# A batched fp32 matmul: the first block of x comes in two halves, one over each DMA queue

## The chip, the cores and the metric

The kernel runs on one core of a Trainium2 chip. The time is device microseconds of that core for one execution, and a kernel's time is the median of its runs. A profile is one execution recorded by the hardware profiler; its times are counted from the span's start.

## The reference

```python
def setup_inputs():
    batch, m, k, n = 32, 512, 1024, 768
    return {
        "x": np.random.randn(batch, m, k).astype(np.float32),
        "weight": np.random.randn(batch, k, n).astype(np.float32),
    }

def reference(x, weight):
    return np.matmul(x, weight).astype(np.float32)
```

There are 32 independent products of a 512 x 1024 matrix with a 1024 x 768 matrix, all in fp32 in HBM. The kernel multiplies in bf16 and sums in fp32.

## The kernel before, in words

**Tiling.** Batches are taken in 16 pairs. The x of one pair (4 MB in fp32) lies over the 128 partitions so that partitions 0 to 63 hold the pair's first batch and partitions 64 to 127 its second (`x_view`, L39). Each partition holds 8 rows of 1024 numbers, which are contiguous in HBM; the 8 rows are the index `mo`. A weight matrix (3 MB in fp32) lies over the 128 partitions with 8 x 768 numbers on each (L37, L38). There are two slots for the x of a pair (`xs`), four for weights (`ws`), and four for results (`outs`, one per pair).

**Loads.** x and weights are wanted in bf16. GpSimd's queue, the software queue, converts while it moves: `load_w` (L93) and `load_x` (L108) read fp32 from HBM and write bf16 to SBUF. The one exception is the x of the first pair. SyncE loads it over the hardware queue, unconverted, into a piece of the result buffer that is not yet in use (`x_first`, L53; issued at L393), and VectorE and ScalarE convert it into `xs[0]`: `cast_first` (L275) lets each engine wait for `s_first` and copy four of the eight `mo`; ScalarE's last copy also waits for `s_cast`, which VectorE raises after its four, and then raises `s_xr`, on which TensorE waits before it touches a pair's x.

**TensorE** (`on_pe`, L192). For each pair: 8 groups of 4 transposes (L174, x seen as 32-bit words, with the identity `ident` as the other operand), which VectorE copies out of PSUM into `both` (`spread`, L217); then for each of the two batches a wait for its weights (`s_wr`) and 4 x 8 pairs of matmuls (L139 and L166). ScalarE (L262, L266) and VectorE (L271, L273) copy the sums out of PSUM into `outs`.

**Order on GpSimd** (`on_pool`, L342). First `load_w(0)`; then the identity (a memset, L344, and an affine_select, L346); then `load_w(1)`, `load_x(1)`, `load_w(2)`, `load_w(3)`. After that, in one fixed order, each later load waits until TensorE has freed its slot, and the stores of finished pairs (L119) are put between the loads, some pairs after their results are ready. ScalarE waits for the store of a slot before it writes it again (`slot_free`, L231). SyncE stores the last two pairs, the last one in four pieces (L376 to L379), and waits for the weights to land on TensorE's behalf (L340).

The two helpers around the first load, as they stand before the change:

```python
def cast_first(eng, copy, rows):
    eng.wait_ge(s_first, 16)
    for mo in rows:
        if mo == 2 * MT - 1:
            eng.wait_ge(s_cast, 1)
        last = copy(xs[0][:, mo], x_first[:, mo])
    return last
...
sp.dma_start(x_first, x_view[0]).then_inc(s_first, 16)
```

Of the kernel before, what the change touches and what calls it, by code (L numbers as in the profile page):

```python
# [12 lines left out]
def kernel(  # L13
# [10 lines left out]
    H = P // 2  # L24
# [10 lines left out]
    pe, dve, act, pool, sp = nc.tensor, nc.vector, nc.scalar, nc.gpsimd, nc.sync  # L35
# [3 lines left out]
    x_view = x.rearrange("(p r) (mi mo) k -> p (r mi) mo k", r=2, mo=2 * MT)  # L39
# [3 lines left out]
    def sbuf(name, shape, dtype):  # L43
        return nc.alloc_sbuf_tensor(name, shape, dtype).ap()

    ident = sbuf("ident", [P, P], F32)
    all_ws = sbuf("w", [P, W_SLOTS // 2, 2, KT, N], BF16)
    ws = [all_ws[:, i // 2, i % 2] for i in range(W_SLOTS)]
    xs = [sbuf(f"x{i}", [P, 2 * MT, K], BF16) for i in range(X_SLOTS)]
# [3 lines left out]
    x_first = all_outs[:, 4 * ROW:4 * ROW + 2 * MT * K].rearrange("p (mo k) -> p mo k", mo=2 * MT)  # L53
# [7 lines left out]
    def sem(name):  # L61
        sems.append(nc.alloc_semaphore(name))
        return sems[-1]

    s_first, s_cast, s_zero, s_ident = (sem(f"s_{n}") for n in ("first", "cast", "zero", "ident"))
    s_w = [sem(f"s_w{i}") for i in range(W_SLOTS)]
    s_x = [sem(f"s_x{i}") for i in range(X_SLOTS)]
    s_wr, s_xr = sem("s_wr"), sem("s_xr")
# [7 lines left out]
    def mm_done(b):  # L76
        return 4 * (b + 1)
# [12 lines left out]
    def together(b):  # L90
        return W_SLOTS <= b < B - 2

    def load_w(b):  # L93
        if together(b):
            if b % 2 == 0:
                pool.wait_ge(s_mm, mm_done(b + 1 - W_SLOTS))
                slots = all_ws[:, b // 2 % 2].rearrange("p r ko n -> p r (ko n)")
                pool.dma_start(out=slots, in_=w_two_view[b // 2]).then_inc(s_w[b % W_SLOTS], 16)  # L98
            return
        if b >= W_SLOTS:  # L100
            pool.wait_ge(s_mm, mm_done(b - W_SLOTS))
        pool.dma_start(out=ws[b % W_SLOTS], in_=w_view[b]).then_inc(s_w[b % W_SLOTS], 16)  # L102
# [5 lines left out]
    def load_x(k):  # L108
        if k >= X_SLOTS:
            pool.wait_ge(s_mm, mm_begun(k - X_SLOTS))  # L110
        pool.dma_start(out=xs[k % X_SLOTS], in_=x_view[k]).then_inc(s_x[k % X_SLOTS], 16)  # L111
# [5 lines left out]
    def store(eng, a, sem):  # L117
        copied(eng, 4 * a + 3)
        eng.dma_start(out=two_view[a], in_=outs[a % OUT_SLOTS]).then_inc(sem, 16)  # L119
# [72 lines left out]
    def on_pe():  # L192


        odd = pe.alloc_register("odd")
        pe.reg_mov(odd, 0)
        pe.wait_ge(s_ident, 1)
        with nc.Fori(0, PAIRS, engines=[mybir.EngineType.PE], hint_back_edge=True):
            take(s_xr)
            for k in range(X_SLOTS):  # L200
                with pe.If_eq(odd, k):
                    transposes(k)
            w_pair = all_ws[:, bass.ds(nc.snap(odd, min_val=0, max_val=1), 1)]
            for b in range(2):
                take(s_wr)
                for mt in range(MT):
                    if b == 0:
                        await_copies(s_c, 2 * mt + 2, GROUPS, GROUPS)
                    at = 2 * b + mt // 2 + 1 + mt % 2
                    await_copies(s_a, at, 5, 4)  # L210
                    await_copies(s_d, at, 5, 4)
                    multiply(b, mt, w_pair[:, 0, b])
            pe.reg_alu(odd, odd, 1, mybir.AluOpType.bitwise_xor)
# [61 lines left out]
    def cast_first(eng, copy, rows):  # L275

        eng.wait_ge(s_first, 16)
        for mo in rows:
            if mo == 2 * MT - 1:
                eng.wait_ge(s_cast, 1)  # L280
            last = copy(xs[0][:, mo], x_first[:, mo])  # L281
        return last

    def on_dve():


        turn = dve.alloc_register("turn")
        dve.reg_mov(turn, 0)
        dve.sem_inc(s_d, 2)
        dve.sem_inc(s_free, OUT_SLOTS)  # L290
        cast_first(dve, dve.tensor_copy, range(MT)).then_inc(s_cast, 1)
        turns = PAIRS // OUT_SLOTS

        def spreads(k, copy):
            for g in range(GROUPS):
                dve.wait_ge(s_pt, GROUPS * k + g + 1)
                copy(g).then_inc(s_c, 1)

        def sets(b):
            dve.wait_ge(s_free, 1).then_inc(s_free, -1)  # L300
            set_on_dve(b, 0)
            set_on_dve(b, 1)
            set_on_dve(b + 1, 0)

        with nc.Fori(0, turns, engines=[mybir.EngineType.DVE], hint_back_edge=True):
            for k in range(OUT_SLOTS - 1):
                spreads(k, spread)
                if k:
                    set_on_dve(2 * k - 1, 1)
                else:  # L310
                    with dve.If_ne(turn, 0):
                        set_on_dve(2 * OUT_SLOTS - 1, 1)
                sets(2 * k)
            k = OUT_SLOTS - 1
            with dve.If_ne(turn, turns - 1):
                spreads(k, spread)
            with dve.If_eq(turn, turns - 1):
                spreads(k, spread_last)
            set_on_dve(2 * k - 1, 1)
            with dve.If_ne(turn, turns - 1):  # L320
                sets(2 * k)
            with dve.If_eq(turn, turns - 1):
                sets(B - 2)
            step = GROUPS * OUT_SLOTS
            dve.wait_ge(s_pt, step).then_inc(s_pt, -step)
            dve.reg_add(turn, turn, 1)
        set_on_dve(B - 1, 1)

    def on_act():
        act.sem_inc(s_a, 2)  # L330
        cast_first(act, act.copy, range(MT, 2 * MT)).then_inc(s_xr, 1)
        for b in range(B):
            out_on_act(b, 0)
            if b % 2 and b < B - 1:
                landed(act, s_x[(b // 2 + 1) % X_SLOTS], (b // 2 + 2) // 2, s_xr)
            out_on_act(b, 1)
# [3 lines left out]
        eng.wait_ge(slot, 16 * n).then_inc(ready, uses)  # L340

    def on_pool():  # L342
        load_w(0)
        pool.memset(ident, 0.0).then_inc(s_zero, 1)  # L344
        pool.wait_ge(s_zero, 1)
        pool.affine_select(  # L346
            out=ident,
            in_=ident,
            compare_op=mybir.AluOpType.not_equal,
            fill=1.0,  # L350
            base=0,
            pattern=[[-1, P]],
            channel_multiplier=1,
        ).then_inc(s_ident, 1)
        load_w(1)
        load_x(1)
        load_w(2)
        load_w(3)
        def stores(first, last):
            for a in range(max(first, 0), last):  # L360
                store(pool, a, s_st[a % OUT_SLOTS])


        for k in range(PAIRS - 2):
            load_x(k + 2)
            if k % 2 == 0:
                stores(k - 3, k - 1)
            load_w(2 * k + 4)
            load_w(2 * k + 5)
        stores(PAIRS - 3 - HELD, PAIRS - 2)  # L370

    def on_sp():
        for b in range(B):
            if not (together(b) and b % 2):
                landed(sp, s_w[b % W_SLOTS], loads_of_w(b), s_wr, 1 + together(b))
        store(sp, PAIRS - 2, s_fin)  # L376
        for b in (B - 2, B - 1):
            for p in range(2):
                store_half(b, p)  # L379
        sp.sem_inc(s_zero, 1)  # L380

    def clear_on_pool():

        for i, s in enumerate(s_st):
            pool.wait_ge(s, 16 * len(range(i, PAIRS - 2, OUT_SLOTS)))
        pool.wait_ge(s_zero, 2)
        used = range(sems[0].num, s_fin.num)
        pool.dma_reset(used)
        pool.sem_clear(used)
        pool.wait_ge(s_fin, 80).then_inc(s_fin, -80)  # L390

    with tc.tile_critical(sync_engine=mybir.EngineType.Activation, no_gpsimd_drain=True):  # L392
        sp.dma_start(x_first, x_view[0]).then_inc(s_first, 16)  # L393
        on_pool()
        on_pe()
        on_dve()
        on_act()
        on_sp()
        clear_on_pool()
# [30 lines left out]
```

## Time and profile before

| what | before |
|---|---|
| median of 3 runs | 512.89 us (512.43 to 513.11) |
| span of the profiled execution | 510.1 us |
| instructions in the span | 5783 |
| TensorE busy | 422.5 us |
| VectorE busy | 212.8 us |
| ScalarE busy | 115.8 us |
| GpSimd busy | 29.0 us |
| mean granted TensorE clock | 0.951 |

The span runs from the first to the last instruction that the profiler recorded. The device time of the profiled execution is not listed by itself; the median of the runs is 2.8 us longer than the span, and that much is taken to lie around it. "DMA share" in a view by windows is the mean busy share of the core's 16 DMA engines (it can pass 1 in a short window, where packets overlap or are put down to the window they began in). GB/s are counted in the bytes as they are written, so a load that converts fp32 to bf16 counts half of what it reads. "PEq", "SPq" and so on are an engine's sequencer. In the DMA rows the tile names tell the transfer: `outs<-in_x_dram` is the first load of x, since `x_first` lies in the result buffer.

### The profile page before, as it was taken

To read this page: it belongs to the slowest core of one execution; us is meant where nothing else is said; L and a number is where in the kernel's file an instruction comes from. 1 tells how busy PE (TensorE), PEld (TensorE's weight loads), DVE (VectorE), ACT (ScalarE), POOL (GpSimd) and SP (SyncE) were. 2 spreads that over 40 slices of the span, in tenths; PEclk is the share of its full clock that TensorE was granted. 3 is DMA by queue.
4 is the path that set the end of the run, shared out by engine and by line. 5 is a ranking of instruction groups with operands and counts; after the bars stand their busy time and mean duration, and the time that the engine had idled before them with its cause. 6 is when DMAs were issued, how large, how long until landed. Compare 5 with 4: busy or idle time off the path is not lost. (4 is left out here: it accounts for less than half of the span.)

```text
span 510.1 us, 5783 instructions
## 1 busy us (share of the span) xinstructions
PE 422.5 (83%) x2512; PEld 172.3 (34%) x1536; DVE 212.8 (42%) x332; ACT 115.8 (23%) x197; POOL 29.0 (6%) x54
## 2 busy tenths in 40 slices
PE   0199999999999599993999939999499984999990
PEld 0143425353525134251343403434144331343420
DVE  0253636454536136351463513635145441454631
ACT  1313131313231221302313023130222302223130
POOL 2000001000100001000010000100001000100000
PEclk9999999999999899997999969999799995999996
DMA  8999999999999999999999999999999999999997
GB/s 296 261 213 216 217 215 220 212 299 251 214 217 224 432 241 218 215 229 432 233 219 216 244 432 216 220 216 259 419 216 218 219 272 405 215 215 236 434 427 336
DMA packets 9443, 136.34 MB, mean 267 GB/s; under 512 B 864, under 2 KB 864, under 8 KB 1376
## 3 DMA queue, kind: packets, MB, share of 16 engines
q0 software_dynamic: 8576, 125.83, 95.7%
q1 hardware_dynamic: 864, 10.49, 5.0%
q14 instruction: 3, 0.02, 0.0%
HBM read 167.77 MB, written 50.33 MB: 428 GB/s over the span
## 5 line engine op out<-in xcount | busy, mean ns | idle before, releaser
L166 PE MATMUL pm<-w,xT 128*128 x976 | 328.2, 386 | 36.3 <-DVE outs L271 36.3
L139 PE MATMUL pm<-w,xT 128*128 x1024 | 283.9, 277 | 4.7 <-DVE xT L220 1.7
L166 PEld LDWEIGHTS pm<-w,xT 128*128 128x128 bf16 x1024 | 101.8, 99 | 275.4 <-issue 235.8
L271 DVE COPY outs<-pm 64x512 f32<-64x512 f32 x128 | 88.1, 688 | 199.8 <-DVEq L269 198.4
L262 ACT COPY outs<-pm 64x512 f32<-64x512 f32 x128 | 74.1, 579 | 264.1 <-PE pm L139 163.2
L174 PE MATMUL pt<-ident,x 128*128 128x128 f32 x512 | 84.5, 307 | 33.4 <-PEq L178 23.1
L220 DVE COPY xT<-pt 128x1024 bf16<-128x1024 bf16 x120 | 77.8, 687 | 63.4 <-PE pt L174 63.0
L174 PEld LDWEIGHTS pt<-ident,x 128*128 128x128 f32 x512 | 71.2, 210 | 48.7 <-issue 26.5
L266 ACT COPY outs<-pm 64x512 f32<-64x512 f32 x64 | 37.0, 578 | 99.9 <-PE pm L139 99.8
L273 DVE COPY outs<-pm 64x512 f32<-64x512 f32 x64 | 43.9, 685 | 0.0
L98 POOL DMA_DIRECT2D w<-in_weight_dram x13 | 9.2, 706 | 260.0 <-PE pm L139 260.0
L111 POOL DMA_DIRECT2D x<-in_x_dram x15 | 8.3, 555 | 127.3 <-PE pm L139 88.7
L281 DVE CAST x<-outs 128x1024 bf16<-128x1024 f32 x4 | 2.5, 690 | 18.9 <-DMA outs<-in_x_dram 18.9
L119 POOL DMA_DIRECT2D out_dram<-outs x14 | 7.5, 537 | 7.1 <-DVE outs L273 7.1
L281 ACT CAST x<-outs 128x1024 bf16<-128x1024 f32 x4 | 3.9, 1042 | 16.6 <-DMA outs<-in_x_dram 16.6
L228 DVE COPY xT<-pt 128x512 bf16<-128x512 bf16 x16 | 5.7, 418 | 4.1 <-PE pt L174 4.1
L102 POOL DMA_DIRECT2D w<-in_weight_dram x6 | 3.4, 564 | 29.1 <-PE pm L139 27.9
L281 ACT ACT_TABLE_LOAD x1 | 1.3, 1283 | 1.0 <-ACTq L392 1.0
L346 POOL TENSOR_SCALAR_AFFINE_SELECT ident<-ident 128x128 f32<-128x128 f32 x1 | 0.3, 282 | 0.2 <-POOL ident L344 0.2
L344 POOL MEMSET ident<- 128x128 f32 x1 | 0.2, 223 | 0.0
L414 POOL MEMSET const-float32-0.0<- 128x1 f32 x1 | 0.1, 98 | 0.2 <-issue 0.2
L414 POOL MEMSET const-bfloat16-1.0<- 128x1 bf16 x1 | 0.1, 102 | 0.0
(2 smaller groups left out, 0.2 us busy)
## 6 DMA issues: line engine op xcount, KB each, us to landing
out_dram<-outs POOLq DMA_DIRECT2D x14, 3072.0 KB, 39.0
w<-in_weight_dram POOLq DMA_DIRECT2D x13, 3072.0 KB, 29.1
x<-in_x_dram POOLq DMA_DIRECT2D x15, 2048.0 KB, 30.4
w<-in_weight_dram POOLq DMA_DIRECT2D x6, 1536.0 KB, 29.8
outs<-in_x_dram SPq DMA_DIRECT2D x1, 4096.0 KB, 18.0
out_dram<-outs SPq DMA_DIRECT2D x1, 3072.0 KB, 18.8
out_dram<-outs SPq DMA_DIRECT2D x4, 768.0 KB, 15.2
```

The costliest lines, as they stand in the source:

```text
L98: pool.dma_start(out=slots, in_=w_two_view[b // 2]).then_inc(s_w[b % W_SLOTS], 16)
L111: pool.dma_start(out=xs[k % X_SLOTS], in_=x_view[k]).then_inc(s_x[k % X_SLOTS], 16)
L119: eng.dma_start(out=two_view[a], in_=outs[a % OUT_SLOTS]).then_inc(sem, 16)
L139: return pe.add_instruction(mybir.InstMatmult(name=nc.get_next_instruction_name(), engine=mybir.EngineType.PE, ins=[pe.lower_ap(moving), p ...
L166: last = pe.matmul(*args, start=(ko == 0), stop=(ko == KT - 1))
L174: last = pe.transpose(pts[g % 2][:, j, :], words[:, mo, j::JT], ident)
L220: return dve.tensor_copy(both[g // 2][:, :, :, g % 2].rearrange("p b j i r -> p j b i r"), pt)
L262: last = act.copy(*piece)
L266: act.copy(*pieces(b, p, 2)[0]).then_inc(s_ap, 1)
L271: last = dve.tensor_copy(*piece)
L273: dve.tensor_copy(*pieces(b, p, 2)[1]).then_inc(s_dp, 1)
L281: last = copy(xs[0][:, mo], x_first[:, mo])
```

## The change

A semaphore `s_rest` is added. SyncE's load of the first x takes partitions 0 to 63 alone, still in fp32 into `x_first`. Partitions 64 to 127 become the software queue's first transfer, ahead of `load_w(0)`, converted on the way into `xs[0]`, where they are needed. The eight converting copies take partitions 0 to 63 alone. ScalarE's last copy also waits for `s_rest`, so that `s_xr` still says that all of the x of the first pair is there.

```diff
-    s_first, s_cast, s_zero, s_ident = (sem(f"s_{n}") for n in ("first", "cast", "zero", "ident"))
+    s_first, s_rest, s_cast, s_zero, s_ident = (
+        sem(f"s_{n}") for n in ("first", "rest", "cast", "zero", "ident")
+    )
...
             if mo == 2 * MT - 1:
                 eng.wait_ge(s_cast, 1)
-            last = copy(xs[0][:, mo], x_first[:, mo])
+                eng.wait_ge(s_rest, 16)
+            last = copy(xs[0][:H, mo], x_first[:H, mo])
...
     def on_pool():
+        pool.dma_start(out=xs[0][H:], in_=x_view[0, H:]).then_inc(s_rest, 16)
         load_w(0)
...
-        sp.dma_start(x_first, x_view[0]).then_inc(s_first, 16)
+        sp.dma_start(x_first[:H], x_view[0, :H]).then_inc(s_first, 16)
```

`H` is 64, half of the partitions.

## The prediction

> **What bounds the kernel now.** I read the page's totals first, then the DMA rows, then the windows of the first 20 us, of the middle and of the end.
>
> ```profile
> span 510.1 us, 5783 instructions
> ...
> PE 422.5 (83%) x2512; PEld 172.3 (34%) x1536; DVE 212.8 (42%) x332; ACT 115.8 (23%) x197; POOL 29.0 (6%) x54
> ...
> DMA  8999999999999999999999999999999999999997
> ...
> HBM read 167.77 MB, written 50.33 MB: 428 GB/s over the span
> ...
> w<-in_weight_dram POOLq DMA_DIRECT2D x13, 3072.0 KB, 29.1
> x<-in_x_dram POOLq DMA_DIRECT2D x15, 2048.0 KB, 30.4
> w<-in_weight_dram POOLq DMA_DIRECT2D x6, 1536.0 KB, 29.8
> outs<-in_x_dram SPq DMA_DIRECT2D x1, 4096.0 KB, 18.0
> ```
>
> No compute engine fills the span; the DMA engines do, in every slice but the first and the last. The software queue's loads are listed at their bf16 size: 13 x 3072 + 15 x 2048 + 6 x 1536 KB is 81.8 MB, twice that plus the 4.19 MB of the first x is the 167.8 MB read.
>
> ```profile
> core 0: us, PE busy (x) PEld busy (x) DVE busy (x) ACT busy (x) POOL busy (x), PEclk, DMA share, GB/s
> 20.00:170.00 150.00, 142.09 (x861) 60.53 (x535) 72.42 (x111) 37.54 (x63) 8.45 (x14) 1.00 1.02 232
> 170.00:180.00 10.00, 4.68 (x17) 1.11 (x8) 1.98 (x3) 2.80 (x5) 0.00 (x0) 0.68 1.00 433
> 250.00:290.00 40.00, 38.20 (x237) 17.20 (x151) 20.61 (x32) 8.68 (x15) 3.60 (x6) 1.00 1.02 217
> 470.00:500.00 30.00, 25.94 (x158) 10.39 (x96) 15.60 (x31) 7.52 (x13) 0.00 (x0) 1.00 1.01 427
> 500.00:508.00 8.00, 0.00 (x0) 0.00 (x0) 0.00 (x0) 0.00 (x0) 0.00 (x0) 0.57 0.93 388
> ```
>
> The DMA share is 1.0 from 20 us to 500 and still 0.93 up to 508. Where stores run, 433 GB/s are written (170 to 180); where mostly converting loads run, 217 GB/s are written (250 to 290), so about 434 read. A converting load therefore costs an engine what its fp32 side costs: **conversion is free, and the time is bytes of fp32 over 428 GB/s**. The queue never runs dry, so whatever time the 16 engines lose at the start comes out at the end, one for one.
>
> TensorE isn't the bound:
>
> ```profile
> PE pm L166 <- DVE outs L271: 36.3, 5, 8.2
> PE pt L174 <- PEq L178: 23.1, 1, 23.1
> ```
>
> These are waits (total, times, longest). Once started at 23.1 us, TensorE later stands still five times, 36.3 us in all, at results whose slots the stores have not freed. A start some us earlier would lengthen those waits.
>
> **The change part by part.** The rows of the start:
>
> ```profile
> 0.93 0.38 SPq L393 DMA_DIRECT2D outs<-in_x_dram  x1
> ...
> 1.49 0.67 POOL L102 DMA_DIRECT2D w<-in_weight_dram  x1 [1.04 <-ACTq L392]
> ...
> 3.62 0.54 POOL L111 DMA_DIRECT2D x<-in_x_dram  x1
> 4.14 1.08 POOL L102 DMA_DIRECT2D w<-in_weight_dram  x2
> 18.92 3.89 ACT L281 CAST x<-outs 128x1024 bf16<-128x1024 f32 x4 [16.60 <-DMA outs<-in_x_dram]
> 18.92 2.50 DVE L281 CAST x<-outs 128x1024 bf16<-128x1024 f32 x4 [18.92 <-DMA outs<-in_x_dram]
> ...
> 23.14 6.87 PE L174 MATMUL pt<-ident,x 128*128 128x128 f32 x32 [23.14 <-PEq L178]
> ...
> 32.84 1.17 ACT L262 COPY outs<-pm 64x512 f32<-64x512 f32 x2 [10.03 <-PE pm L139]
> ...
> 33.10 0.53 POOL L111 DMA_DIRECT2D x<-in_x_dram  x1 [27.88 <-PE pm L139]
> ```
>
> ```profile
> 0.00:2.00 2.00, 0.00 (x0) 0.00 (x0) 0.00 (x0) 0.96 (x1) 0.71 (x5) 1.00 0.31 82
> 2.00:4.00 2.00, 0.00 (x0) 0.00 (x0) 0.00 (x0) 0.32 (x1) 1.59 (x5) 1.00 0.87 279
> 4.00:6.00 2.00, 0.00 (x0) 0.00 (x0) 0.00 (x0) 0.00 (x0) 1.22 (x3) 1.00 1.00 426
> 6.00:8.00 2.00, 0.00 (x0) 0.00 (x0) 0.00 (x0) 0.00 (x0) 0.00 (x0) 1.00 1.08 360
> 8.00:10.00 2.00, 0.00 (x0) 0.00 (x0) 0.00 (x0) 0.00 (x0) 0.00 (x0) 1.00 1.04 344
> ```
>
> From 4 to 6 us the rate is 426, that of unconverted bytes alone: only SyncE's transfer moves. From 6 on it falls, as bytes that count half join: the software queue's first data comes at about 6 us, 4.5 after its issue began.
>
> 1. **Bytes**: 2.10 MB of fp32 pass from one queue to the other. Both cost their fp32 side: 2.10 / 0.426 = 4.92 us of all engines either way. Net 0.
>
> 2. **GpSimd's extra issue**: between 0.54 us (x at 3.62) and 0.67 (the first at 1.49), ahead of everything in its order. `load_w(0)`, the identity and the four other issues slip by as much; the last now ends at 5.22. The identity, made before the issue at 3.62, is needed at 23.14; the weights queue behind the x half; GpSimd then idles until 33.10. Net 0; without that cover, 0.6 us.
>
> 3. **The first software data**: what covers its lead is SyncE's transfer. By 6.0 us that has moved 2 x (82 + 279 + 426) KB = 1.57 MB (some program code in the first row), as if at full rate since 2.3 us. Its half would last to 2.3 + 4.92 = 7.2 at full rate, 1.2 us past the first software data. No gap, net 0; if the lead grew, each us over 1.2 costs one.
>
> 4. **Casts and waits**: eight casts remain. No row has a 64-partition cast; bounds are half of the present times (half the elements) and all of them (equal columns). I take all, 3.89 and 2.50 us, since column counts are unchanged. The new wait on `s_rest` stands before ScalarE's last cast only; behind it are `s_xr`, thus TensorE's first transposes, and the first result copy at 32.84, which has waited 10.03 us. The x half lands before the weights behind it in its queue. All of this moves TensorE's start, which has 36.3 us of later waits to give. Net 0 at the end.
>
> 5. **The rate of a transfer that writes 64 partitions.** This decides. All rows are of transfers over 128 partitions. The highest rate that they show into or out of SBUF is 433 GB/s, 3.4 per partition; the fp32 load at 426 is 3.3. On the new path 64 partitions would have to take 426 GB/s, 6.7 each, which no row shows. The bounds are 426, as now, and 213, the same rate per partition. The rate per partition is what the rows have shown, so I take 213. Up to 6.0 us, SyncE's half then moves for 3.7 us at half speed: **1.85 us lost**, 0.79 MB moved, 1.31 MB left. Afterwards the engines alternate between it and the other half. That one writes bf16: at 426 GB/s read it writes 213 into 64 partitions, 3.3 each, so it needs no more than rows show. The remaining 1.31 MB lose between nothing (an engine held up at one half leaves its share to an engine that is at the other) and 1.31/0.213 - 1.31/0.426 = 3.07 us (they keep step). While two queues take turns, the share of 1.04 to 1.08 says that an engine has hardly more than one packet under way, so a slow packet holds its engine up: nearer to the upper end. I take two thirds, **2.05 us**.
>
> [...]
>
> **Sum**: 0 + 0 + 0 + 0 + 1.85 + 2.05 = +3.9 us. Against the profiled span: 510.1 + 3.9 = 514.0; against the median, with the same 2.8 us around it: 512.89 + 3.9 = **516.8 us**, between 514.7 (1.85 lost) and 517.8 (4.92).
>
> **The rivals.**
>
> *A 64-partition write runs at full rate; no difference.* For it: the engines pass 26.7 GB/s each (428 / 16) whatever they move, in 433 and in 217 GB/s rows, so they themselves may be the limit. Against it: 6.7 GB/s per partition is unseen. Then all terms are 0: 512.9, within 512.3 and 513.5.
>
> *TensorE's earlier start reaches the end; faster.* Both halves would have come by 2.3 + 2 x 4.92 = 12.1 us, landing about 13.5 instead of 18.92, so TensorE starts 5.4 us sooner; if the chain from there to the last store set the time, 507.5. It decides as soon as a DMA engine runs dry waiting for slots that TensorE frees. Against it: share 1.0 throughout, and a share of 0.93 from 500 to 508, where TensorE does nothing. For it: GpSimd's load at 33.10 had waited 27.88 us for TensorE, though with other loads still queued.
>
> *The upper half is slowed as well*, because it too writes 64 partitions: then 4.92 + 4.92 = +9.8, 522.7. Against it: in bf16 it asks no more of a partition than rows show. [...]
>
> *The software queue's first data comes late*, past 7.2 us: by 9.2 it would leave the engines idle for 2 us: 514.9, if the lower half is not slow (if it is, it covers this gap). For it: the lead is one reading, 4.5 us. Against it: the same issue is first in the same queue.
>
> **How the numbers follow.** Chances: forecast 0.60, no difference 0.23, faster by the earlier start 0.05, both halves slow 0.06, late software data 0.06. Beyond 0.2% (1.03 us, about what a measurement of this kernel can tell from no change): faster 0.06, with 0.01 from the edge of the no-difference case; same 0.22; slower 0.72. The forecast's own range is 514.7 to 517.8. To leave no more than 2 in 10 out, the range goes down into the no-difference case, to 512.6, which takes in most of it and the late data, and up to 518.2; outside stay both halves slow, the faster case and the lower edge of no difference, some 0.18 together.
>
> **What would show it.** In the changed profile the window from 4 to 6 us should show a DMA share near 1.0 at some 215 to 260 GB/s in place of 426; at 400 or over, term 5 is wrong. SyncE's load, now 2048 KB, should need 12 to 15 us to land; at full rate it would be 7 to 9. The software half (1024 KB) should land at about 17 us (2.3 + 2 x 4.92 + 3.9 is 16.0, and about a us to landing); at full rate about 13.5. TensorE should start at 18 to 20 us, so earlier than 23.1, and yet the last store come later; its waits at L166 should grow by about what it gains at the start plus what is lost. The first weights should land some 4 us later. Windows from 30 to 500 should keep share 1.0. A share well under 1 anywhere between 4 and 500, or an end that follows TensorE's start, would overturn the reading that the DMA engines bound it.

## The result, and the profile after

| kernel | median, us | runs | span of the profiled execution, us |
|---|---|---|---|
| before | 512.43 (511.97 to 513.11) | 5 | 510.1 |
| after | 517.06 (515.79 to 517.2) | 5 | 515.1 |

The changed kernel is slower: the ratio is 1.0088, 95% interval 1.0077 to 1.0099. That is 4.63 us between the medians and 5.0 us between the profiled spans.

The page of the changed kernel, its totals, then its two loads of the first x among the DMA rows (KB each, us from issue to landing):

```profile
span 515.1 us, 5833 instructions
...
DMA  8999999999999999999999999999999999999997
...
HBM read 167.77 MB, written 50.33 MB: 423 GB/s over the span
...
outs<-in_x_dram SPq DMA_DIRECT2D x1, 2048.0 KB, 15.3
x<-in_x_dram POOLq DMA_DIRECT2D x1, 1024.0 KB, 17.1
```

The bytes are the same to the last digit and the DMA row is as full as before; they only took 5 us longer. SyncE moved half of what it moved before and still needed 15.3 us, where all of it had needed 18.0.

The start, first the timeline of the changed kernel, then its windows, whose last two columns are DMA share and GB/s:

```profile
0.93 0.56 SPq L397 DMA_DIRECT2D outs<-in_x_dram  x1
...
1.49 0.64 POOL L346 DMA_DIRECT2D x<-in_x_dram  x1 [1.04 <-ACTq L396]
2.13 0.56 POOL L104 DMA_DIRECT2D w<-in_weight_dram  x1
...
16.27 3.89 ACT L284 CAST x<-outs 64x1024 bf16<-64x1024 f32 x4 [13.95 <-DMA outs<-in_x_dram]
16.27 2.49 DVE L284 CAST x<-outs 64x1024 bf16<-64x1024 f32 x4 [16.27 <-DMA outs<-in_x_dram]
...
20.50 6.47 PE L176 MATMUL pt<-ident,x 128*128 128x128 f32 x28 [20.50 <-PEq L180]
```

```profile
2.00:4.00 2.00, 0.00 (x0) 0.00 (x0) 0.00 (x0) 0.32 (x1) 1.62 (x5) 1.00 1.12 262
4.00:6.00 2.00, 0.00 (x0) 0.00 (x0) 0.00 (x0) 0.00 (x0) 1.72 (x4) 1.00 1.28 262
6.00:8.00 2.00, 0.00 (x0) 0.00 (x0) 0.00 (x0) 0.00 (x0) 0.00 (x0) 1.00 1.28 262
8.00:10.00 2.00, 0.00 (x0) 0.00 (x0) 0.00 (x0) 0.00 (x0) 0.00 (x0) 1.00 0.35 74
```

A packet seems to be counted in the window in which it begins: three windows in a row have exactly 262 GB/s, 16 packets of 32 KB each (524 KB in 2 us), and then one has 74. So these short windows are read together. From 2 to 9.4 us, first the kernel before, then the changed one:

```profile
2.00:9.40 7.40, 0.00 (x0) 0.00 (x0) 0.00 (x0) 0.32 (x1) 2.81 (x7) 1.00 0.95 328
```

```profile
2.00:9.40 7.40, 0.00 (x0) 0.00 (x0) 0.00 (x0) 0.32 (x1) 3.34 (x8) 1.00 1.01 215
```

The engines are as busy and move a third less, although 48 of the 49 packets of that window are unconverted and count in full. **Busy engines at 215 GB/s, where unconverted bytes alone passed at 426 before** (4 to 6 us), is the whole finding; it has to be read from the rate, since the share of busy time hides it.

The trace's records of single packets say it packet by packet. A packet here is the 32 KB row of one partition: SyncE's half is 64 packets, all of it before was 128. The records don't name the engine, so the packets are taken 16 at a time in the order of their starts. The second 16 begin where the first end (after: at 4.89 us, and 2.58 + 2.31 is 4.89), so they are read as one packet at a time on each of the 16 engines, four of SyncE's half on each (eight before). Medians of each 16, in us:

```
SyncE's packet of an engine   1st    2nd    3rd    4th
before                        1.93   1.23   1.23   1.23
after                         2.31   2.56   2.56   2.31
first packet begins: before 2.08, after 2.58
first software packet begins: before 6.50, after 9.98
converted 32 KB rows of the other half (after): 1.23 to 1.25 each
```

The four packets take 9.74 us in place of 5.62, so 4.1 us are lost in them, and 0.5 more because the first begins later (0.34 for the earliest of the 16): 4.6 us, as much as the medians differ. Sixteen packets of 32 KB in 2.56 us are 205 GB/s; the 215 of the window takes in the quicker first packets, and one converted packet that had only begun.

TensorE's waits and the windows of the end, after; then the last window of the kernel before:

```profile
PE pm L168 <- DVE outs L273: 41.5, 5, 9.1
PE pt L176 <- PEq L180: 20.5, 1, 20.5
...
PE pm L168 <- PEq L180: 2.9, 1, 2.9
```

```profile
470.00:500.00 30.00, 29.26 (x182) 11.56 (x107) 15.62 (x31) 7.54 (x13) 0.00 (x0) 1.00 1.01 397
500.00:508.00 8.00, 2.77 (x18) 0.69 (x8) 1.98 (x3) 1.74 (x3) 0.00 (x0) 0.96 0.97 412
508.00:512.00 4.00, 0.00 (x0) 0.00 (x0) 0.00 (x0) 0.00 (x0) 0.00 (x0) 0.50 0.90 375
```

```profile
508.00:512.00 4.00, 0.00 (x0) 0.00 (x0) 0.00 (x0) 0.00 (x0) 0.00 (x0) 0.50 0.01 5
```

TensorE starts 2.6 us earlier than before (20.5 against 23.1), then waits 5.2 us longer for results that the stores have not freed, and a wait of 2.9 us is new. Transfers now run on past 508 us, at 375 GB/s, where before almost nothing was left (5).

### The profile page after: what moved, and what is told of

It is laid out like the page before. It is cut to its first block, busy times and chain, and to the rows that moved or that the text cites. A ratio compares the mean times of both kernels' runs of the same rounds, so it can differ in the third digit from the quotient of the medians.

```text
span 515.1 us, 5833 instructions
## 1 busy us (share of the span) xinstructions
PE 427.0 (83%) x2560; PEld 172.7 (34%) x1536; DVE 212.9 (41%) x332; ACT 116.1 (23%) x197; POOL 29.5 (6%) x55
## 3 DMA queue, kind: packets, MB, share of 16 engines
HBM read 167.77 MB, written 50.33 MB: 423 GB/s over the span
## 5 line engine op out<-in xcount | busy, mean ns | idle before, releaser
L168 PE MATMUL pm<-w,xT 128*128 x1024 | 343.4, 387 | 45.0 <-DVE outs L273 41.5
L141 PE MATMUL pm<-w,xT 128*128 x1024 | 283.3, 277 | 0.0
L176 PE MATMUL pt<-ident,x 128*128 128x128 f32 x512 | 84.9, 309 | 30.8 <-PEq L180 20.5
L284 DVE CAST x<-outs 64x1024 bf16<-64x1024 f32 x4 | 2.5, 680 | 16.3 <-DMA outs<-in_x_dram 16.3
L284 ACT CAST x<-outs 64x1024 bf16<-64x1024 f32 x4 | 3.9, 1043 | 14.0 <-DMA outs<-in_x_dram 14.0
## 6 DMA issues: line engine op xcount, KB each, us to landing
outs<-in_x_dram SPq DMA_DIRECT2D x1, 2048.0 KB, 15.3
x<-in_x_dram POOLq DMA_DIRECT2D x1, 1024.0 KB, 17.1
```

What stands on the lines that cost most here:

```text
L141: return pe.add_instruction(mybir.InstMatmult(name=nc.get_next_instruction_name(), engine=mybir.EngineType.PE, ins=[pe.lower_ap(moving), p ...
L168: last = pe.matmul(*args, start=(ko == 0), stop=(ko == KT - 1))
L176: last = pe.transpose(pts[g % 2][:, j, :], words[:, mo, j::JT], ident)
L284: last = copy(xs[0][:H, mo], x_first[:H, mo])
```

## The experiments

Each was timed beside the kernel before on the same chip; the three batches had the kernel before at 512.17, 512.01 and 512.16 us. In what follows a transfer is called narrow when it goes to 64 partitions or fewer, and wide when it goes to all 128. The theory to test: fp32 written into 64 partitions holds its DMA engines up twice as long, and what they lose at the start comes out at the end. The main rival: the cost lies in the order of the software queue (a new first transfer, one more issue, the weights behind it). The other: an earlier TensorE is worth something.

**The same division by rows instead of partitions.** SyncE loads 4 of the 8 rows of all 128 partitions, the software queue the others; VectorE and ScalarE convert two rows each.

```diff
-        pool.dma_start(out=xs[0][H:], in_=x_view[0, H:]).then_inc(s_rest, 16)
+        pool.dma_start(out=xs[0][:, MT:], in_=x_view[0, :, MT:]).then_inc(s_rest, 16)
...
-        sp.dma_start(x_first[:H], x_view[0, :H]).then_inc(s_first, 16)
+        sp.dma_start(x_first[:, :MT], x_view[0, :, :MT]).then_inc(s_first, 16)
```

> The same division of the first x between the two queues, 2.1 MB each and the software half first in its queue, but by rows mo instead of by partitions: SyncE loads mo 0 to 3 of all 128 partitions, the software queue mo 4 to 7 of all 128. Theory (the cost is that fp32 written into 64 partitions passes at about half rate): no transfer is narrow, so the cost goes: 512.4 us within 1 us, SyncE's load lands within about 9 us of its issue in place of 15.3, the windows from 4 us on show some 426 GB/s until software data joins. Rival (the cost comes from the new first software transfer, its extra DMA or the weights behind it): all of that is kept, so 516 to 517.5. Rival (an earlier start of TensorE shortens the run): TensorE starts some 8 us earlier than before, so 505 to 508.

Measured: 511.96 us, ratio to the kernel before 0.9993 (0.9984 to 1.0002). From its page, SyncE's load and TensorE's first wait:

```profile
outs<-in_x_dram SPq DMA_DIRECT2D x1, 2048.0 KB, 9.8
```

```profile
PE pt L176 <- PEq L180: 14.6, 1, 14.6
```

Both queues carry what they carry in the change, in the same order, and the cost is gone. That refutes the order. TensorE starts 8.5 us earlier than before and the time doesn't move: that refutes the gain from its start. 9.8 us to land is a little more than the expected 9.

**Two narrow halves on the hardware queue**, with the software queue as it was before.

```diff
-        eng.wait_ge(s_first, 16)
+        eng.wait_ge(s_first, 32)
...
-        sp.dma_start(x_first, x_view[0]).then_inc(s_first, 16)
+        sp.dma_start(x_first[:H], x_view[0, :H]).then_inc(s_first, 16)
+        sp.dma_start(x_first[H:], x_view[0, H:]).then_inc(s_first, 16)
```

> The kernel before with one edit: SyncE's load of the first x is issued as two transfers, partitions 0 to 63 and then 64 to 127, both fp32 on the hardware queue. GpSimd's queue is as before. Theory: both transfers are narrow and fp32, 4.9 us are lost in each, 512.4 + 9.8 = 522 us (over 519 in any case), and the x lands at about 27 us in place of 18.9. Rival (the cost of the change comes from the software queue's order): 512.4, or 0.1 to 0.6 us more for one more issue.

Measured: 521.05 us, ratio 1.0166 (1.0153 to 1.0180), 8.9 us more than before. Its window from 2 to 9.4 us:

```profile
2.00:9.40 7.40, 0.00 (x0) 0.00 (x0) 0.00 (x0) 0.32 (x1) 2.81 (x7) 1.00 0.98 214
```

The cost appears without any change to the software queue, and twice the narrow bytes cost about twice as much, some 1 us less than the 522 expected. By the packet records (medians) its eight packets took 18.6 us in place of 10.5 and the first began 0.9 later: 8.9. The casts began at 28.7 us, where the data were expected at about 27.

**Two narrow halves on the software queue, converted**; no load on SyncE, no converting copies.

```diff
+        pool.dma_start(out=xs[0][:H], in_=x_view[0, :H]).then_inc(s_rest, 16)
         pool.dma_start(out=xs[0][H:], in_=x_view[0, H:]).then_inc(s_rest, 16)
...
-        sp.dma_start(x_first[:H], x_view[0, :H]).then_inc(s_first, 16)
```

> No load of x on SyncE and no converting copies: both halves of the first x (64 partitions each) are the software queue's first two transfers, converted on the way. Theory: converted data are written at half the bytes, so narrow transfers cost nothing; what is left is the software queue's lead, during which no data move: first data between 3.5 and 6 us in place of 2.2, so 513.5 to 516.5, with the windows after the first data at DMA share 1.0 and about 213 GB/s written. Rival (any transfer into 64 partitions is slow): the same lead and 9.8 us more: 523 to 526, with some 107 GB/s written in the first 20 us.

Measured: 513.41 us, ratio 1.0027 (1.0016 to 1.0039). It lies just under the range; the first data came at 3.1 us (packet records), earlier than expected. The rows of 32 KB took 1.23 to 1.25 us after the first, as the wide converted ones of the kernel before do (1.23, median of 1920): these narrow transfers that write bf16 aren't slowed. They read the same rows from HBM as the two slow halves above (8.9 us lost), so the cost isn't on the side of reading.

**The same as one converting load of 128 partitions**, to tell the width from the start (the edit is against the run just told).

```diff
-        pool.dma_start(out=xs[0][:H], in_=x_view[0, :H]).then_inc(s_rest, 16)
-        pool.dma_start(out=xs[0][H:], in_=x_view[0, H:]).then_inc(s_rest, 16)
+        pool.dma_start(out=xs[0], in_=x_view[0]).then_inc(s_rest, 16)
```

> As the run with two software halves, but the first x is one converting load over all 128 partitions in the software queue; nothing on SyncE, no converting copies. Theory (converted narrow loads cost nothing extra): the same as with two halves, 513.4 within 0.6; what both have over 512.2 is the software queue's later first data (3.1 us in place of 2.2). Rival (part of that 1.2 us was the narrow halves): 512.2 to 512.6.

Measured: 512.90 us, ratio 1.0017 (1.0008 to 1.0026), first data at 3.0 us. The ratios of this run and the last differ by 0.0010, half a us, and their intervals overlap, so no cost of the width is shown here. Both begin to move data 0.9 to 1.0 us later than the kernel before, which is most of what they cost (0.9 and 1.2).

**A quarter in place of a half.** SyncE loads partitions 0 to 31, the software queue the other 96.

```diff
-            last = copy(xs[0][:H, mo], x_first[:H, mo])
+            last = copy(xs[0][:H // 2, mo], x_first[:H // 2, mo])
...
-        pool.dma_start(out=xs[0][H:], in_=x_view[0, H:]).then_inc(s_rest, 16)
+        pool.dma_start(out=xs[0][H // 2:], in_=x_view[0, H // 2:]).then_inc(s_rest, 16)
...
-        sp.dma_start(x_first[:H], x_view[0, :H]).then_inc(s_first, 16)
+        sp.dma_start(x_first[:H // 2], x_view[0, :H // 2]).then_inc(s_first, 16)
```

> The change with 32 partitions in place of 64: SyncE loads partitions 0 to 31 (1.05 MB fp32), the software queue 32 to 127 (converted). Theory with the limit at groups of partitions that 64 and 32 partitions share: 32 pass at the same 213 GB/s as 64, so half the bytes lose half the time, 2.5 us: 514.9. Theory with the limit at the single partition (3.3 GB/s each): 107 GB/s, 1.05/0.107 - 1.05/0.426 = 7.4 us lost: 519.8. Rival (order of the software queue): as the change, 517.

Measured: 513.79 us, ratio 1.0026 (1.0015 to 1.0037), so 1.6 us between medians. The two packets of an engine took 2.39 and 2.56 us (packet records), much as with 64 partitions (2.31 and 2.56); a limit of so many GB/s for each partition would have made them twice as long again. That form of the theory, the one in the prediction, falls. The 2.5 us expected were too many by the first packet, which is slow in any case (1.93 before): 0.46 + 1.33 = 1.8.

**The price of narrow bytes by themselves.** Three kernels leave the kernel before as it is and load 2.10 MB more in fp32, which nothing uses, behind the first load: into partitions 0 to 63, into half the columns of all 128, or into the middle 64 (one line each, in this order). In all three ScalarE waits for the load before its first result copy.

```diff
+        sp.dma_start(x_more[:H], x_view[1, :H]).then_inc(s_rest, 16)
...
+        sp.dma_start(x_more[:, :MT], x_view[1, :, :MT]).then_inc(s_rest, 16)
...
+        sp.dma_start(x_more[H // 2:3 * H // 2], x_view[1, H // 2:3 * H // 2]).then_inc(s_rest, 16)
```

Partitions 0 to 63:

> The kernel before, and behind its first load SyncE loads 2.10 MB more in fp32 (data that nothing uses, into result columns that are written only from 32 us on) into partitions 0 to 63; ScalarE waits for it before its first result copy. Theory: the bytes cost 2.10/0.426 = 4.9 us as any others, and being narrow they hold their engines up besides. In the run with two narrow halves the pair of them lost 8.9 us, so one of them some 4.4: 512.2 + 4.9 + 4.4 = 521.5 us. Rival (width plays no part, time goes by bytes alone): 517.1.

All 128:

> The same 2.10 MB more in fp32 from the same queue, but as 4 of the 8 rows of all 128 partitions. Both theories: 512.2 + 4.9 = 517.1 us. It shows whether engine time added at the start comes out at the end one for one (then 517.1), or is partly taken up by slack (under 516).

The middle 64:

> The same 2.10 MB more in fp32, into 64 partitions again, but the middle ones, 32 to 95. Theory in its first form (so many GB/s per partition, so any 64 partitions are slow): as the run with partitions 0 to 63, 521.5. Theory with the limit at shared paths: the run with 32 partitions lost less than the one with 64 and not four times as much as bytes, so partitions 0 to 31 and 32 to 63 seem to share paths; partitions 64 to 95 then have others, and the middle 64 reach all paths: 517.1, no extra loss. [...]

Measured: 521.42 us (ratio 1.0183, 1.0169 to 1.0196), 516.85 (1.0095, 1.0079 to 1.0110) and 516.76 (1.0096, 1.0080 to 1.0111). The window from 19 to 30 us of the three, in this order:

```profile
19.00:30.00 11.00, 6.75 (x34) 5.43 (x34) 7.21 (x12) 3.62 (x4) 0.00 (x0) 1.00 0.95 201
```

```profile
19.00:30.00 11.00, 6.92 (x33) 5.62 (x33) 6.83 (x12) 3.51 (x4) 0.00 (x0) 1.00 1.01 304
```

```profile
19.00:30.00 11.00, 6.98 (x33) 5.37 (x33) 7.21 (x12) 3.58 (x4) 0.00 (x0) 1.00 0.99 292
```

These rates mix fp32 packets with converted ones, which count half. By the packet records the four packets of an engine into partitions 0 to 63 took 2.08, 2.39, 2.55 and 2.38 us, those into the middle 64 took 1.21 to 1.23.

Three readings. The wide 2.10 MB cost 4.84 us for 4.92 us of engine time (2.10 MB at 426 GB/s): what is added at the start comes out at the end one for one. The bytes into partitions 0 to 63 cost 4.57 us on top, and their packets are 4.5 us longer. And 64 partitions need not be slow: the middle 64 cost no more than all 128. It is not how many partitions are written but which.

**The change with the middle 64 on SyncE**, partitions 0 to 31 and 96 to 127 on the software queue.

```diff
-        pool.dma_start(out=xs[0][H:], in_=x_view[0, H:]).then_inc(s_rest, 16)
+        pool.dma_start(out=xs[0][:H // 2], in_=x_view[0, :H // 2]).then_inc(s_rest, 16)
+        pool.dma_start(out=xs[0][3 * H // 2:], in_=x_view[0, 3 * H // 2:]).then_inc(s_rest, 16)
...
-        sp.dma_start(x_first[:H], x_view[0, :H]).then_inc(s_first, 16)
+        sp.dma_start(x_first[H // 2:3 * H // 2], x_view[0, H // 2:3 * H // 2]).then_inc(s_first, 16)
```

> The change with other partitions: SyncE loads the middle 64 (32 to 95) in fp32, the software queue loads 0 to 31 and 96 to 127, converted, as its first two transfers; 16 casts of 32 partitions in place of 8 of 64. The software queue's order, the bytes per queue and the 64 partitions of the hardware transfer are as in the change; a transfer and eight casts more. Theory (partitions 0 to 63 share half of the paths into SBUF, and that is the whole cost): 512.1 within 0.7 us; SyncE's load lands within some 10 us of its issue in place of 15.3. Rival (a part of the 4.6 us has to do with the order or the split as such): between 513.5 and 517.

Measured: 512.95 us, ratio 1.0017 (1.0008 to 1.0026). Its window from 2 to 9.4 us, and SyncE's load:

```profile
2.00:9.40 7.40, 0.00 (x0) 0.00 (x0) 0.00 (x0) 0.32 (x1) 3.83 (x9) 1.00 1.05 354
```

```profile
outs<-in_x_dram SPq DMA_DIRECT2D x1, 2048.0 KB, 10.0
```

Some 4 of the 4.6 us go. The 0.8 that stays is a little more than the 0.7 allowed for: the first packet begins at 2.5 us, 0.4 later than before, but takes 1.64 us, so that the second begins 0.2 later (4.23 against 4.04, packet records); the rest isn't settled.

**The halves exchanged.** SyncE loads partitions 64 to 127, the software queue 0 to 63.

```diff
-            last = copy(xs[0][:H, mo], x_first[:H, mo])
+            last = copy(xs[0][H:, mo], x_first[H:, mo])
...
-        pool.dma_start(out=xs[0][H:], in_=x_view[0, H:]).then_inc(s_rest, 16)
+        pool.dma_start(out=xs[0][:H], in_=x_view[0, :H]).then_inc(s_rest, 16)
...
-        sp.dma_start(x_first[:H], x_view[0, :H]).then_inc(s_first, 16)
+        sp.dma_start(x_first[H:], x_view[0, H:]).then_inc(s_first, 16)
```

> The change with its halves exchanged: SyncE loads partitions 64 to 127 in fp32, the software queue 0 to 63, converted. Theory (the upper 64 share the other half of the paths): as the change, 516.5 to 517.3. Rival (the lower partitions alone are slow to write, for what else lies there): 512.1 within 0.7 us.

Measured: 516.53 us, ratio 1.0082 (1.0069 to 1.0096). The window from 2 to 9.4 us has the share and the rate of the change:

```profile
2.00:9.40 7.40, 0.00 (x0) 0.00 (x0) 0.00 (x0) 0.33 (x1) 3.33 (x8) 1.00 1.01 215
```

**The two narrow halves on two hardware queues.** As the run with two halves on SyncE, but ScalarE issues the upper one (the edit is against that run).

```diff
         sp.dma_start(x_first[:H], x_view[0, :H]).then_inc(s_first, 16)
-        sp.dma_start(x_first[H:], x_view[0, H:]).then_inc(s_first, 16)
+        act.dma_start(x_first[H:], x_view[0, H:]).then_inc(s_first, 16)
```

> As the run with two narrow halves on SyncE (521.05 us), but the upper half is issued by ScalarE, so the two narrow fp32 transfers lie on two hardware queues and the engines can take turns between them. If the engines stay in step (all write the lower half, then all the upper), nothing is hidden: 520 to 522. If they drift apart, so that some write the lower half while others write the upper, the paths are all in use: 512.5 to 516.

Measured: 521.12 us, ratio 1.0163 (1.0149 to 1.0177), as with one queue:

```profile
2.00:9.40 7.40, 0.00 (x0) 0.00 (x0) 0.00 (x0) 0.92 (x1) 2.82 (x7) 1.00 1.01 219
```

The engines keep step to within 1.3 us (packet records): two packets of the lower half come first, then one of the upper, then both halves in turns with software packets between, and after the first packet each takes 2.3 to 2.6 us in either half.

Taken together, by the packet records a packet of 32 KB in fp32 took 2.39 and 2.56 us into partitions 0 to 31, 2.31 to 2.56 into 0 to 63, 2.3 to 2.6 after the first into 64 to 127, but 1.21 to 1.23 into 32 to 95 and 1.23 into all 128. That fits a division in which partitions 0 to 31 and 32 to 63 share one limit, near 205 GB/s (16 packets in 2.56 us), 64 to 127 have another, and 32 to 95 draw on both. It is a reading of these rates: no run loads 32 to 63 or 64 to 95 alone, and none shows what lies behind the limits. The "paths" of the expectations were the author's assumption, which no run shows. The last run adds that the two narrow halves, issued on two hardware queues, hid nothing of each other's cost (521.12 us, 521.05 with one queue), and the run with the middle 64 showed the full rate in a transfer that goes to only half of the partitions.

## Why the prediction was right, and where it was off

The forecast was 516.8 us and +3.9; measured were 517.06 and +4.63. That the two times lie only 0.3 us apart is in part luck: the forecast started from 512.89, the median of three runs, and the kernel before came out at 512.43 over five. By the prediction's own steps:

- **What bounds the kernel.** Right, and shown: engine time added at the start comes out in full (4.84 of 4.92 us), and an earlier TensorE is worth nothing (8.5 us earlier, ratio 0.9993).
- **Steps 1 and 4, bytes and casts.** Right: 167.77 MB read again; casts of 3.89 and 2.49 us with half the partitions.
- **Step 2, GpSimd's issue.** Right in size (0.64 us, the weights 0.64 later). The least time to landing among the single weight loads went from 19.2 to 23.0 us, so the weights came about 4.4 us later, for the reason of step 5.
- **Step 3, the first software data.** No gap opened, but the reading behind it was wrong. "4.5 after its issue began" was taken for the queue's lead. With nothing on SyncE the first software data came at 3.1 us; before and after alike they came behind each engine's third hardware packet (6.5 and 10.0 us). What looked like a latency was a place in a line.
- **Step 5, the rate.** The bound chosen, 213 GB/s, was right; measured 205 to 215. Its reason, a rate per partition, was not: a quarter ran at the same rate (2.39 and 2.56 us a packet) and the middle 64 at full rate (1.21 to 1.23). The two terms were mis-sized by the error of step 3: the half moved alone up to 10.0 us, not 6.0, and lost 0.38 + 1.33 + 1.33 = 3.0 us in three packets, not 1.85; beside software data it lost 1.1 us in its last packet, not 2.05. The two errors nearly cancelled, which is luck. The choice of "two thirds" for what is lost beside software data was somewhat low: the last packet lost 1.1 of a possible 1.33 us, and in the run with two halves on SyncE the packets beside software data lost 0.9 to 1.1. The first packet's later start, 0.5 us, was not foreseen; with it the parts, 3.0 + 1.1 + 0.5, give the 4.6.
- **Rivals.** No difference, the earlier start and late software data didn't happen. Both halves slow didn't either: the converted half ran at 1.23 us a row.
- **What would show it.** The window from 4 to 6 us read 262, two above its bound, for the counting told above. SyncE's landing took 15.3 us against 12 to 15, the software half landed at 1.49 + 17.1 = 18.6 against 17, TensorE started at 20.5 against 18 to 20: late by 0.3, 1.6 and 0.5 us, where the sum lacked 0.7. TensorE's waits grew by 5.2 + 2.9 = 8.1 us; expected was what it gained at the start plus what was lost, 2.6 + 4.6 to 5.0, so 7.2 to 7.6.

## What to carry to other kernels

Here the DMA engines were busy from the first byte to the last, and only what cost engine time counted (4.84 of 4.92 us added came out at the end, a TensorE 8.5 us earlier gave nothing). Read the rate beside the busy share: engines held up by where they wrote showed as busy (share 1.01 at 215 GB/s, where the kernel before had 0.95 at 328). Before a load is divided, ask into which partitions each part goes: by columns over all 128 it cost nothing (ratio 0.9993), by halves of the partitions 4.6 us, with the middle 64 on SyncE 0.8. The first arrival behind other traffic wasn't the queue's latency (6.5 us, and 3.0 to 3.1 without that traffic); take the other traffic away before calling it that.

## What the runs showed of the hardware that was not expected

- 64-partition fp32 writes were slow into 0 to 63 and into 64 to 127 (2.0 to 2.6 us for a packet of 32 KB) and not into 32 to 95 (1.21 to 1.23 after the first).
- Where three or more hardware packets of 32 KB waited, the software packets began only after three of them for each engine, whether these took 1.23 or 2.56 us (6.5 and 10.0 us); with packets of 16 KB, in the division by rows, after five (5.9 us). Software data alone began at 3.0 to 3.1 us.
- SyncE's issue of the first load took 0.56 us for 64 partitions against 0.38 for 128, and its first packet began 0.5 us later; why is open.
